# Latent attention: the products with the values in runs of six, behind the exponentials of three blocks of keys

## The chip, the cores and the metric

One Trainium2 chip, one of its cores. The metric is the time of one execution of the whole program on the device, in microseconds, as the median of several runs. The core has five engines that work side by side, each with its own queue of instructions in a fixed order: TensorE (PE in the rows; PEld is its loading of weights), VectorE (DVE), ScalarE (ACT), GpSimd (POOL) and SyncE (SP), whose queue issues the DMA transfers. An instruction starts when it stands first in its engine's queue and the semaphores that it waits for are there.

## The reference

Two transformer-like blocks over 512 latent and 256 context tokens of width 1024, in float32. The part that is changed is the attention of the first block's second layer: 16 heads, 512 queries, 768 keys, head width 96 for the scores and 64 for the values.

```python
def softmax_attention(q, k, v):
    s = jnp.einsum('bqhd,bkhd->bhqk', q, k).astype(jnp.float32) * ((QK_NOPE + QK_ROPE) ** -0.5)
    p = jax.nn.softmax(s, axis=-1)
    return jnp.einsum('bhqk,bkhd->bqhd', p.astype(v.dtype), v)
```

## The kernel before

The work is laid out with the keys on the partitions. The heads go in eight pairs (`p` = 0 to 7). `attend(p)` runs over six blocks of 128 keys; for each block and each head `i` of the pair it makes the transposed scores [128 keys, 512 queries] in one bank of PSUM by three products of split operands (high and low parts, lines 1607 to 1609), and ScalarE writes their exponentials (`act`, line 382) to one half of a buffer `pt` in SBUF. The two products with the values (line 1614) follow, one for each head. A product writes 64 partitions: the first head's the lower half of the bank `po`, the second head's the upper half. They sum over the blocks in `po`. The exponentials of the blocks are also added up (line 385): blocks 1, 4 and 5 into the buffer of block 0 on VectorE, block 3 into the buffer of block 2 on GpSimd. After the last block four products with a column of ones (line 1624, the "sum" below) give the row sums, VectorE takes the reciprocal (line 1627, 3.36 us) and multiplies `po` by it.

While a pair is attended to, `project(p + 1)` makes the next pair's operands from other banks: weights are split and multiplied (lines 430, 432, 435), queries and keys are split again, and a bound on each query's scores is found: 16 products (line 1583), each two of them followed by a reduction of 768 columns on VectorE (line 1584), then a small cast (line 1586) and eight transposing products (line 1590, 1x128 in the order) whose row enters the next pair's scores. Three of the eight banks belong to `attend` (one is `po`, two take scores by turns), five to the rest.

The lines are written in the order of the mathematics; a scheduler places the instructions on each engine by its own estimate of when operands are there, which is how the products of line 1583 and those of the projection come to stand between the score products. Once it has run, the order on each engine is fixed. A float32 product on 64 columns of the array is two MATMUL instructions in the trace, so the 96 products with the values are 192 instructions of 512 columns.

Of the kernel before, what the change touches and what calls it, by code (L numbers as in the profile page):

```python
# [11 lines left out]
AF = mybir.ActivationFunctionType  # L12
OP = mybir.AluOpType
# [3 lines left out]
TL, TC, TA = 512, 256, 768  # L17
# [343 lines left out]
class _K:  # L361
# [18 lines left out]

    def act(self, out, in_, func=AF.Copy, **kw):
        return self.nc.scalar.activation(out, in_, func, **kw)  # L382

    def tt(self, out, a, b, op, eng=None):
        return (eng or self.nc.vector).tensor_tensor(out, a, b, op=op)  # L385
# [1028 lines left out]
    def mla(self, a, vec):  # L1414
        nc, A, B, I = self.nc, self.A, self.B, self.I
        A.forget(9999)
        mm = nc.tensor.matmul
# [36 lines left out]
        acc = A.new([TA], top=True)  # L1454
# [18 lines left out]
        b = B.new()  # L1473
# [19 lines left out]
        sc = 96.0 ** -0.5  # L1493
# [102 lines left out]
        def attend(p, ops):  # L1596

            qh, ql, kh, kl = ops
            v = vs[p // 2]
            po = B.new()  # L1600
            acc = [None, None]
            for kb in range(6):
                ks = slice(128 * kb, 128 * kb + 128)
                pt = A.new([2, TL])
                for i in range(2):
                    b = B.new()
                    mm(b.a, kh.a[:97, i, ks], qh.a[:97, i, :], start=True, stop=False)  # L1607
                    mm(b.a, kl.a[:96, i, ks], qh.a[:96, i, :], start=False, stop=False)
                    mm(b.a, kh.a[:96, i, ks], ql.a[:96, i, :], start=False, stop=True)
                    self.act(pt.a[:, i, :], b.a, AF.Exp, scale=sc)  # L1610
                    b.free()
                for i in range(2):
                    h = 2 * (p % 2) + i
                    mm(po.a[64 * i:64 * i + 64, :], v.a[:, kb, 64 * h:64 * h + 64], pt.a[:, i, :], start=(kb == 0), stop=(kb == 5))  # L1614
                j = 1 if kb in (2, 3) else 0
                if acc[j] is None:
                    acc[j] = pt
                else:
                    self.tt(acc[j].a, acc[j].a, pt.a, OP.add, nc.gpsimd if j else None)
                    pt.free()  # L1620
            b = B.new()
            for j in range(2):
                for i in range(2):
                    mm(b.a[64 * i:64 * i + 64, :], self.ones.a[:, :64], acc[j].a[:, i, :], start=(j == 0), stop=(j == 1))
            self.free(acc)
            r = A.new([TL])
            nc.vector.reciprocal(r.a, b.a)
            b.free()
            self.tt(o.a[:, p, :], po.a, r.a, OP.mult)
            self.free([r, po, qh, ql])  # L1630
            if p % 2:
                v.free()
# [3 lines left out]
        for p in range(8):  # L1636
            nxt = project(p + 1) if p < 7 else None
            if p == 6:
                A.limit = 20480 // A.G
                self.wraw = [self.load(I["w1out"][n], "inner") for n in range(2, 2 + 6)]  # L1640
                A.limit = A.n
            B.cur = 3
            attend(p, ops)
            self.in_zone(0)
            ops = nxt
# [1093 lines left out]
```

## Time and profile before

| what | value |
|---|---|
| median of 3 runs | 3063.88 us (3060.31 to 3068.25) |
| the profiled execution, own time | 3062.72 us |
| its span, first to last instruction | 3061.0 us |
| TensorE busy in the span | 94% |
| VectorE, ScalarE, GpSimd busy | 56%, 32%, 10% |
| mean granted TensorE clock, share of full speed | 0.964 |

The attention over the eight pairs lies between 1246 and 1510 us of the span. Busy time counts an engine as busy while one of its instructions runs; for TensorE the ends of pipelined products are modelled, so that a product of 512 columns is shown with 0.39 to 0.40 us while the next starts some 0.23 us after it. Distances between starts say more than durations.

### The profile page before, as it was taken

To read this page: it belongs to the slowest core of one execution; us is meant where nothing else is said; L and a number is where in the kernel's file an instruction comes from. 1 tells how busy PE (TensorE), PEld (TensorE's weight loads), DVE (VectorE), ACT (ScalarE), POOL (GpSimd) and SP (SyncE) were. 2 spreads that over 40 slices of the span, in tenths; PEclk is the share of its full clock that TensorE was granted. 3 is DMA by queue.
4 is the path that set the end of the run, shared out by engine and by line. 5 is a ranking of instruction groups with operands and counts; after the bars stand their busy time and mean duration, and the time that the engine had idled before them with its cause. 6 is when DMAs were issued, how large, how long until landed. Compare 5 with 4: busy or idle time off the path is not lost.

```text
span 3061.0 us, 43732 instructions
## 1 busy us (share of the span) xinstructions
PE 2879.1 (94%) x17880; PEld 2056.7 (67%) x17880; DVE 1703.4 (56%) x2733; ACT 982.3 (32%) x1605; POOL 297.6 (10%) x271
## 2 busy tenths in 40 slices
PE   7989999999999989999999999979798898999997
PEld 4776557888888877555588787877585564344443
DVE  5856547686575354656664784368856943121113
ACT  5522334511211256333453522254322323010011
POOL 0134310000000010111100000010301311000000
PEclk9999999999999999999999999989898887999999
DMA  6334362366465131001222222213113135999998
GB/s 217 103 109 123 117 198 71 124 232 201 134 234 184 34 118 42 23 26 42 90 84 84 82 90 70 89 36 124 63 50 104 48 132 189 399 409 409 409 409 295
DMA packets 170585, 458.99 MB, mean 150 GB/s; under 512 B 20320, under 2 KB 52704, under 8 KB 170000
## 3 DMA queue, kind: packets, MB, share of 16 engines
q1 hardware_dynamic: 170384, 456.19, 42.6%
q8 instruction: 140, 2.29, 0.3%
q14 instruction: 61, 0.50, 0.1%
HBM read 441.35 MB, written 14.78 MB: 149 GB/s over the span
## 4 chain that ended last, share of the span: by engine, by line
PE 69%; DVE 10%; DMA 5%; issue 4%; ACT 3%; POOL 1%; SPq 0%; DVEq 0%; ACTq 0%; POOLq 0%
PE ps L430 13%; PE ps L432 13%; PE ps L435 13%; PE ps L2596 9%; DVE mem L385 5%; ACT mem L382 3%; PE ps L1614 3%; PE ps L2579 2%; DVE mem L388 1%; DMA mem<-in_wadt_dram 1%; PE ps L606 1%; PE ps L1607 1%; PE ps L1770 1%; PE ps L1583 1%; POOL mem L385 1%
## 5 line engine op out<-in xcount | busy, mean ns | idle before, releaser
L382 ACT ACTIVATE mem<-mem 128x1024 fp32r<-128x1024 f32 (+16 forms) x802 | 543.5, 707 | 876.0 <-PE ps L435 224.0
L385 DVE TENSOR_TENSOR mem<-mem,mem 128x1024 fp32r<-128x1024 f32 (+13 forms) x595 | 508.5, 871 | 380.6 <-ACT mem L382 188.0
L382 ACT ACTIVATE mem<-ps 128x512 f32<-128x512 f32 (+8 forms) x607 | 313.1, 529 | 1026.5 <-PE ps L435 327.1
L430 PE MATMUL ps<-mem,mem 128*128 128x512 f32 (+3 forms) x1991 | 598.2, 357 | 14.8 <-ACT mem L382 10.2
L432 PE MATMUL ps<-mem,mem 128*128 128x512 f32 (+2 forms) x1906 | 567.5, 353 | 1.0 <-DVE mem L385 0.9
L435 PE MATMUL ps<-mem,mem 128*128 128x512 f32 (+2 forms) x1977 | 416.3, 351 | 0.0
L430 PEld LDWEIGHTS ps<-mem,mem 128*128 128x128 f32 (+2 forms) x1991 | 338.7, 189 | 86.6 <-ACT mem L382 17.0
L432 PEld LDWEIGHTS ps<-mem,mem 128*128 128x128 f32 (+1 forms) x1906 | 325.2, 188 | 59.9 <-issue 5.9
L435 PEld LDWEIGHTS ps<-mem,mem 128*128 128x128 f32 (+1 forms) x1977 | 322.7, 189 | 56.2 <-issue 4.1
L2596 PE MATMUL ps<-mem,mem 128*64 128x512 f32 x1344 | 308.4, 599 | 1.1 <-ACT mem L382 0.5
L432 PE MATMUL ps<-mem 128*128 128x512 f32 (+1 forms) x814 | 272.2, 364 | 1.3 <-POOL mem L385 0.9
L430 PE MATMUL ps<-mem 128*128 128x512 f32 (+1 forms) x729 | 254.4, 373 | 11.8 <-ACT mem L382 7.9
L385 POOL TENSOR_TENSOR mem<-mem 128x256 f32<-128x256 f32 (+4 forms) x72 | 96.1, 1336 | 1706.5 <-ACT mem L382 1382.7
L385 DVE TENSOR_TENSOR mem<-mem,ps 128x512 f32<-128x512 f32 (+5 forms) x234 | 128.9, 582 | 202.6 <-PE ps L2596 103.4
L385 DVE TENSOR_TENSOR mem<-mem 128x256 f32<-128x256 f32 (+19 forms) x347 | 186.1, 543 | 76.9 <-ACT mem L382 39.0
L2596 PEld LDWEIGHTS ps<-mem,mem 128*64 128x64 f32 x1344 | 106.4, 137 | 177.5 <-issue 164.6
L385 POOL TENSOR_TENSOR mem<-mem,mem 128x512 f32<-128x512 f32 (+6 forms) x104 | 141.4, 1371 | 537.6 <-ACT mem L382 427.5
L385 DVE TENSOR_TENSOR mem<-ps,mem 128x512 f32<-128x512 f32 (+6 forms) x196 | 123.0, 643 | 99.4 <-PE ps L1107 35.4
L432 PEld LDWEIGHTS ps<-mem 128*128 128x128 f32 x814 | 152.5, 194 | 30.2 <-issue 4.4
L435 PE MATMUL ps<-mem 128*128 128x512 f32 (+3 forms) x743 | 171.1, 360 | 0.0
L430 PEld LDWEIGHTS ps<-mem 128*128 128x128 f32 x729 | 139.0, 195 | 44.2 <-ACT mem L382 13.0
L388 DVE SCALAR_TENSOR_TENSOR mem<-ps,mem 128x256 f32<-128x256 f32 (+1 forms) x232 | 114.5, 532 | 73.5 <-PE ps L435 73.2
(301 smaller groups left out, 2930.2 us busy)
## 6 DMA issues: line engine op xcount, KB each, us to landing
mem<-in_eg_dram SPq DMA_DIRECT2D x128, 512.0 KB, 10.2
mem<-in_eu_dram SPq DMA_DIRECT2D x128, 512.0 KB, 10.2
mem<-in_ed_dram SPq DMA_DIRECT2D x128, 512.0 KB, 10.2
mem<-in_wadt_dram SPq DMA_DIRECT2D x96, 512.0 KB, 4.4
mem<-in_wup_dram SPq DMA_DIRECT2D x44, 512.0 KB, 3.6
mem<-in_wgate_dram SPq DMA_DIRECT2D x44, 512.0 KB, 3.5
mem<-in_wdown_dram SPq DMA_DIRECT2D x40, 512.0 KB, 3.5
mem<-in_w2in_dram SPq DMA_DIRECT2D x35, 512.0 KB, 3.7
```

Of the source, the lines that this page charges most:

```text
L382: return self.nc.scalar.activation(out, in_, func, **kw)
L385: return (eng or self.nc.vector).tensor_tensor(out, a, b, op=op)
L388: return self.nc.vector.scalar_tensor_tensor(out, a, s, b, op0=op0, op1=op1)
L430: mm(o, w(0, k), acts[k][0][:, ts], start=(k == 0), stop=False)
L432: mm(o, w(0, k), acts[k][1][:, ts], start=False, stop=False)
L435: mm(o, w(1, k), acts[k][0][:, ts], start=False, stop=(k == nk - 1))
L606: nc.tensor.matmul(b.a[32 * q:32 * q + 32, :], cs.a[:, k, :], raw.a[:, j * 512:(j + 1) * 512], start=(k == 0), stop=(k == 7))
L1583: mm(b.a[:, t0:t1], qh.a[:96, i, 128 * c:128 * c + 128], kh.a[:96, i, t0:t1], start=True, stop=True)
L1607: mm(b.a, kh.a[:97, i, ks], qh.a[:97, i, :], start=True, stop=False)
L1614: mm(po.a[64 * i:64 * i + 64, :], v.a[:, kb, 64 * h:64 * h + 64], pt.a[:, i, :], start=(kb == 0), stop=(kb == 5))
L2579: mm(b.a[:, :256], ht.a[:, c, fs], o, start=(c == 0), stop=(c == 3))
L2596: mm(bk.a[64 * i:64 * i + 64, 512 * n:512 * n + 512], lhs(k, i), w[i][:, 512 * n:512 * n + 512], start=(k == 0), stop=(k == 7))
```

## The change

For each half of a pair's six blocks, all six score blocks (three blocks, two heads) and their exponentials now come first. Then the six products with the values are issued one behind the other, the two heads by turns, at high priority for the scheduler, and each of the six gets an explicit dependency on the last of the six exponentials (`behind`). The additions of the exponentials come after the six products. No instruction is added or taken away.

```diff
+    def behind(self, ins, other):
+
+        self.tc.add_manual_dep(ins.ins, other.ins.name, mybir.DependencyInfo(mybir.DependencyClass.Sync, mybir.DependencyReason.DATA),
+                               reason="in one run")
...
-            for kb in range(6):
-                ks = slice(128 * kb, 128 * kb + 128)
-                pt = A.new([2, TL])
-                for i in range(2):
...
-                    self.act(pt.a[:, i, :], b.a, AF.Exp, scale=sc)
-                    b.free()
-                for i in range(2):
-                    h = 2 * (p % 2) + i
-                    mm(po.a[64 * i:64 * i + 64, :], v.a[:, kb, 64 * h:64 * h + 64], pt.a[:, i, :], start=(kb == 0), stop=(kb == 5))
-                j = 1 if kb in (2, 3) else 0
...
+            for k0 in range(0, 6, 3):
+                pts = []
+                for kb in range(k0, k0 + 3):
...
+                        e = self.act(pt.a[:, i, :], b.a, AF.Exp, scale=sc)
+                        b.free()
+                    pts.append(pt)
+
+                with self.tc.high_priority():
+                    for kb, pt in zip(range(k0, k0 + 3), pts):
+                        for i in range(2):
+                            h = 2 * (p % 2) + i
+                            m = mm(po.a[64 * i:64 * i + 64, :], v.a[:, kb, 64 * h:64 * h + 64], pt.a[:, i, :], start=(kb == 0), stop=(kb == 5))
+                            self.behind(m, e)
+                for kb, pt in zip(range(k0, k0 + 3), pts):
+                    j = 1 if kb in (2, 3) else 0
...
```

Lines shift: the scores' products stand in lines 1614 to 1616 of the changed kernel, those with the values in 1625, the sum in 1637, the bound's products in 1588 (of before 1583) and its transposes in 1595, the projection's in 435, 437 and 440.

TensorE's queue in the first half of pair 4, before: two score products, products of line 1583 for the next pair's bound between them, and the two heads' products with the values apart from each other.

```order
L1607 MATMUL ps<-mem_80,mem_76 128x512
L1608 MATMUL ps<-mem_80,mem_76 128x512
L1583 MATMUL ps<-mem_76,mem_80 128x256
L1609 MATMUL ps<-mem_80,mem_76 128x512
L1614 MATMUL ps<-mem_7557,mem_68 64x512
L1583 MATMUL ps<-mem_76,mem_80 128x512
L1583 MATMUL ps<-mem_76,mem_80 128x256
L1614 MATMUL ps<-mem_7557,mem_68 64x512
L1607 MATMUL ps<-mem_80,mem_76 128x512
```

The same place in the changed kernel, from the last score product of the sixth head (the first row) on; the next two rows of scores belong to the seventh.

```order
L1616 MATMUL ps<-mem_80,mem_76 128x512
L1614 MATMUL ps<-mem_80,mem_76 128x512
L1588 MATMUL ps<-mem_76,mem_80 128x512
L1588 MATMUL ps<-mem_76,mem_80 128x256
L1615 MATMUL ps<-mem_80,mem_76 128x512
L1625 MATMUL ps<-mem_7557,mem_68 64x512 x4
L1625 MATMUL ps<-mem_68 64x512 x2
L1588 MATMUL ps<-mem_76,mem_80 128x512
L1588 MATMUL ps<-mem_76,mem_80 128x256
L1588 MATMUL ps<-mem_76,mem_80 128x512
L1588 MATMUL ps<-mem_76,mem_80 128x256
```

The six products with the values, one or two to a place before, stand in one piece, with two score products and two of the bound's between them and the last score product they need.

TensorE's queue at the end of the same pair, before, from the scores of the twelfth and last head to the sum (1624).

```order
L1607 MATMUL ps<-mem_80,mem_76 128x512
L1608 MATMUL ps<-mem_80,mem_76 128x512
L1609 MATMUL ps<-mem_80,mem_76 128x512
L430 MATMUL ps<-mem_76 128x512
L1614 MATMUL ps<-mem_7557,mem_68 64x512 x2
L432 MATMUL ps<-mem_76 128x512
L430 MATMUL ps<-mem_76 128x256
L430 MATMUL ps<-mem_76 128x512
L432 MATMUL ps<-mem_76 128x256
L432 MATMUL ps<-mem_76 128x512
L1624 MATMUL ps<-mem_7557,mem_64 64x512 x2
L1624 MATMUL ps<-mem_68,mem_64 64x512 x2
```

And in the changed kernel, from the last score product on.

```order
L1616 MATMUL ps<-mem_80,mem_76 128x512
L435 MATMUL ps<-mem_76 128x512
L437 MATMUL ps<-mem_76 128x512
L435 MATMUL ps<-mem_76 128x512
L437 MATMUL ps<-mem_76 128x256
L437 MATMUL ps<-mem_76 128x512
L440 MATMUL ps<-mem_76,mem_80 128x256
L440 MATMUL ps<-mem_76,mem_80 128x512
L1625 MATMUL ps<-mem_7557,mem_68 64x512 x6
L1637 MATMUL ps<-mem_7557,mem_64 64x512 x2
L1637 MATMUL ps<-mem_68,mem_64 64x512 x2
```

The second run stands right in front of the sum, behind seven products of the projection; before, a pair of products with the values stood there, and five of the projection between it and the sum.

The SP queue behind the last pair, before (`w1out` is the weight of the product that follows attention, `wgate` and `cx` belong to later work).

```order
L400 DMA mem_7557<-in_w1out_dram 128x1024 x2
L400 DMA mem_9545<-in_wgate_dram 128x1024
L2138 DMA mem_64<-in_cx_dram 128x256 x3
L400 DMA mem_7557<-in_w2in_dram 128x1024
```

And in the changed kernel.

```order
L405 DMA mem_7557<-in_w1out_dram 128x1024
L405 DMA mem_9545<-in_wgate_dram 128x1024
L2151 DMA mem_64<-in_cx_dram 128x256
L405 DMA mem_7557<-in_w1out_dram 128x1024
L2151 DMA mem_64<-in_cx_dram 128x256 x4
```

The second of the two `w1out` transfers has moved behind a `wgate` transfer and one of `cx`.

## Rows read from the trace of the kernel before

**Rows 1.** the page: the span, TensorE, and the chain that ended last by line.

```profile
span 3061.0 us, 43732 instructions
...
PE 2879.1 (94%) x17880; PEld 2056.7 (67%) x17880; DVE 1703.4 (56%) x2733; ACT 982.3 (32%) x1605; POOL 297.6 (10%) x271
...
PE ps L430 13%; PE ps L432 13%; PE ps L435 13%; PE ps L2596 9%; DVE mem L385 5%; ACT mem L382 3%; PE ps L1614 3%; PE ps L2579 2%; DVE mem L388 1%; DMA mem<-in_wadt_dram 1%; PE ps L606 1%; PE ps L1607 1%; PE ps L1770 1%; PE ps L1583 1%; POOL mem L385 1%
```

**Rows 2.** busy time by engine of two stretches: us (instructions); granted clock; DMA.

```profile
1317.00:1388.00 71.00, 70.73 (x265) 38.59 (x264) 43.09 (x49) 25.71 (x44) 12.30 (x11) 1.00 0.09 27
1388.00:1459.00 71.00, 70.37 (x266) 38.56 (x266) 43.19 (x48) 25.11 (x43) 12.81 (x11) 1.00 0.14 45
```

**Rows 3.** groups of instructions by line from 1240 to 1510 us.

```profile
L1614 PE MATMUL ps<-mem,mem 128*64 128x512 f32 x168 | 77.9, 629 | 1.0 <-ACT mem L382 0.8
...
L1624 PE MATMUL ps<-mem,mem 128*64 128x512 f32 x64 | 15.5, 605 | 0.5 <-DVE mem L385 0.5
...
L1614 PE MATMUL ps<-mem 128*64 128x512 f32 x24 | 11.2, 618 | 0.0
```

**Rows 4.** the timeline, TensorE and ScalarE, 1424.2 to 1429.3 us: start, duration in us.

```profile
1424.26 0.50 PE L1607 MATMUL ps<-mem,mem 97*128 97x512 f32 x1
...
1424.60 0.40 PE L1608 MATMUL ps<-mem,mem 96*128 96x512 f32 x1
...
1425.19 0.39 PE L1609 MATMUL ps<-mem,mem 96*128 96x512 f32 x1
...
1425.67 0.60 ACT L382 ACTIVATE mem<-ps 128x512 f32<-128x512 f32 x1 [1.85 <-PE ps L1609]
...
1425.77 0.40 PE L1608 MATMUL ps<-mem,mem 96*128 96x512 f32 x1
...
1426.01 0.40 PE L1609 MATMUL ps<-mem,mem 96*128 96x512 f32 x1
...
1426.34 1.07 PE L1614 MATMUL ps<-mem,mem 128*64 128x512 f32 x2
...
1427.34 0.97 PE L1583 MATMUL ps<-mem,mem 96*128 96x512 f32 x4
...
1428.24 1.07 PE L1614 MATMUL ps<-mem,mem 128*64 128x512 f32 x2
```

**Rows 5.** the timeline of TensorE around one sum, 1407 to 1410 us.

```profile
1407.72 1.94 PE L1624 MATMUL ps<-mem,mem 128*64 128x512 f32 x8
1409.59 0.97 PE L435 MATMUL ps<-mem,mem 128*128 128x256 f32 x4
```

**Rows 6.** the waits in 1246 to 1508 us: total us, times, longest.

```profile
PEld ps L1614 <- ACT mem L382: 27.2, 70, 0.9
```

**Rows 7.** the timeline of GpSimd, VectorE and TensorE, 1293 to 1297 us.

```profile
1293.67 2.35 POOL L385 TENSOR_TENSOR mem<-mem 128x1024 f32<-128x1024 f32 x1 [12.63 <-issue]
1293.70 2.35 DVE L1586 CAST mem<-mem 128x8 fp32r<-128x8 f32 x1
...
1296.10 0.64 PE L1590 MATMUL ps<-mem,mem 128*1 128x128 f32 x8 [1.01 <-DVE mem L1586]
```

**Rows 8.** the timeline of the SP queue at the end of attention.

```profile
1493.20 8.48 SPq L400 DMA_DIRECT2D mem<-in_w1out_dram  x2
1501.73 0.42 SPq L400 DMA_DIRECT2D mem<-in_wgate_dram  x1
1506.24 1.28 SPq L2138 DMA_DIRECT2D mem<-in_cx_dram  x3
```

**Rows 9.** the timeline of TensorE, 1472 to 1484 us, idle time in brackets.

```profile
1472.76 1.56 PE L1614 MATMUL ps<-mem,mem 128*64 128x512 f32 x4 [0.51 <-ACT mem L382]
...
1483.61 0.80 PE L1607 MATMUL ps<-mem,mem 97*128 97x512 f32 x1 [3.46 <-DVE mem L1627]
```

**Rows 10.** the stretches around and behind these two, columns as in 2.

```profile
1471.80:1478.20 6.40, 5.17 (x16) 1.84 (x15) 4.29 (x6) 3.50 (x7) 0.00 (x0) 1.00 0.02 2
...
1483.60:1489.20 5.60, 5.59 (x11) 2.49 (x11) 1.38 (x2) 1.82 (x3) 0.00 (x0) 0.50 0.26 94
```

More of the change, by code (lines that the diff above doesn't have):

```diff
@@ L1601, in attend @@
             acc = [None, None]
-            for kb in range(6):
-                ks = slice(128 * kb, 128 * kb + 128)
-                pt = A.new([2, TL])
-                for i in range(2):
[L1606 to L1609, printed above, removed]
-                    self.act(pt.a[:, i, :], b.a, AF.Exp, scale=sc)
-                    b.free()
-                for i in range(2):
-                    h = 2 * (p % 2) + i
-                    mm(po.a[64 * i:64 * i + 64, :], v.a[:, kb, 64 * h:64 * h + 64], pt.a[:, i, :], start=(kb == 0), stop=(kb == 5))
-                j = 1 if kb in (2, 3) else 0
[L1616 to L1620, printed above, removed]
+            for k0 in range(0, 6, 3):
+                pts = []
+                for kb in range(k0, k0 + 3):
+                    ks = slice(128 * kb, 128 * kb + 128)
+                    pt = A.new([2, TL])
+                    for i in range(2):
+                        b = B.new()
+                        mm(b.a, kh.a[:97, i, ks], qh.a[:97, i, :], start=True, stop=False)
+                        mm(b.a, kl.a[:96, i, ks], qh.a[:96, i, :], start=False, stop=False)
+                        mm(b.a, kh.a[:96, i, ks], ql.a[:96, i, :], start=False, stop=True)
+                        e = self.act(pt.a[:, i, :], b.a, AF.Exp, scale=sc)
[3 more added lines that the diff above has]
+                    for kb, pt in zip(range(k0, k0 + 3), pts):
+                        for i in range(2):
+                            h = 2 * (p % 2) + i
[3 more added lines that the diff above has]
+                    j = 1 if kb in (2, 3) else 0
+                    if acc[j] is None:
+                        acc[j] = pt
+                    else:
+                        self.tt(acc[j].a, acc[j].a, pt.a, OP.add, nc.gpsimd if j else None)
+                        pt.free()
```

## The prediction

> **What bounds the kernel now.** The page first: TensorE is busy 94% of the span, and the chain that ended last runs mostly over its products [rows 1]. The products with the values (line 1614) hold 3% of that chain, the scores' first product 1%; so the change touches a small part, but a part on the path. Next the busy time by stretch: in the two stretches of 71 us that each cover two pairs, TensorE is busy over 70 us at full clock, VectorE 43 us, ScalarE 25 to 26 us, GpSimd 12 to 13 us [rows 2]. Attention is bound by TensorE's queue, and time saved there is saved at the end as long as the other engines keep up.
>
> Then the groups by line: the products with the values are busy 77.9 + 11.2 = 89.1 us for 192 instructions, the eight sums 15.5 us for 64 [rows 3]. Per instruction that is 0.46 us against 0.24 us, for the same shape, 64 columns of the array and 512 moving columns. The timeline says why. In the sum, eight instructions of two heads by turns take from 1407.72 to 1409.59, 1.87 us [rows 5]. One product with the values that stands alone, two instructions, keeps TensorE from 1426.34 to 1427.34, 1.00 us, and the second head's, after four other products, again 1.00 us from 1428.24 [rows 4]. So instructions of the two heads run side by side, those of one head do not. In TensorE's order before, 34 of the 96 products stand alone and 31 times the two heads' stand together (34 + 62 = 96), where the second head's has to wait for an exponential of its own: TensorE's loading of weights waits for ScalarE 70 times, 27.2 us in all, in part behind products that still run [rows 6].
>
> **The change part by part.** *Side by side.* Busy time of a run grows from 1.07 us (two steps of one head) to 1.94 us (four steps of two heads) [rows 4, 5], so a further step costs (1.94 - 1.07)/2 = 0.435 us. A run of six products is twelve instructions, six steps: 1.07 + 4 x 0.435 = 2.81 us. Sixteen such runs are 45.0 us, against 89.1: 44.1 us less. Each run's busy time overhangs the next start by 0.07 us (1.07 shown, 1.00 to the next start [rows 4]); 65 runs become 16, so 49 x 0.07 = 3.4 us of this was never TensorE's time. 40.7 us remain.
>
> *Changing over.* From one score product to the next it is 0.24 us (1425.77 to 1426.01); from the last one into the run it is 0.33 us (1426.01 to 1426.34), and the first product after a run holds 0.34 us (1424.26 to 1424.60) [rows 4]. A run costs 0.09 + 0.10 = 0.19 us beside its own steps. 49 runs fewer: 9.3 us.
>
> *The sum joins the second run* (the order at the end of pair 4). It loses its own changing over, 0.19 us, and its slot goes from 1.87 us to four steps, 1.74 us: 0.32 us, eight times 2.6 us.
>
> That is 40.7 + 9.3 + 2.6 = 52.6 us gross. Against it stand four new waits.
>
> *The last exponential.* Behind the last score product of the sixth head it takes 0.39 us to its end, then 0.09, the exponential 0.60, and 0.07 to the product: 1425.19 to 1426.34, 1.15 us [rows 4]. 0.24 us are the product's own slot, so other products must fill 0.91 us. In the changed order two score products and two of the bound's (0.24 + 0.24 + 0.24 + 0.12) fill 0.84 in the first run of pairs 1 to 6, and four to seven products of the projection fill all of it in the second run of pairs 0 to 5. Uncovered: 0.4 us once in pair 0, 0.1 six times, 0.2 in pair 7, and 0.9 us in the second runs of pairs 6 and 7, where nothing stands between. Sum 3.0 us. What is queued behind the waiting product (the next head's third score product, the bound's products) waits with it, and VectorE's first addition waits for the run's first two products, since it writes into block 0's exponentials. Both have slack: the sums of exponentials are needed only at line 1624, two blocks' additions later.
>
> *Two banks for scores.* Before, products with the values stood between every two heads. Now six heads' scores come in a row, and the third head's needs the first one's bank, free 1.15 us after its last product's start. TensorE would be there after four slots, 4 x 0.23 = 0.92 us: 0.23 us short. One product between covers it. In the order some 17 of 96 heads have none, most in pair 7 (nine), where there is no next pair to project: 17 x 0.23 = 3.9 us. The other bound is 80 x 0.23 = 18.4 us (96 heads less the 16 behind a run), if fillers don't help.
>
> *The bound's chain on VectorE.* Reductions, additions and the cast come closer together. The nearest row for a bad case: the cast took 2.35 us, as long as a GpSimd addition that began with it, and the transposing products waited 1.01 us for it [rows 7]. GpSimd's addition of block 3 now begins later, near the cast in each pair. I take 0.8 us for six pairs (pair 0 has its wait already), 4.8 us, between 0 and 1.5 us each (9 us).
>
> *The transfers behind attention.* The `w1out` transfers were issued at 1493.2 and 1501.7 (8.48 us for the two issues), `cx` at 1506.2 [rows 8]. The second now stands behind a `wgate` and one `cx`; if those still wait, it comes 4.5 us later against work that comes earlier. I take 2 us, between 0 and 8. A late second block is covered by the products with the first, and by the last pair's reciprocal, on which TensorE waits anyway (3.46 us behind the pair before [rows 9]).
>
> Holding three blocks of exponentials needs more buffers; no row shows a product or exponential that waits for one, so nothing; without that cover, each run would wait for one addition.
>
> New waits: 3.0 + 3.9 + 4.8 + 2 = 13.7 us. Net 52.6 - 13.7 = 38.9 us. On the profiled execution's own 3062.72 us (span and 1.7 us around it) that gives 3023.8, so **3024 us**; the median shown, 3063.88, is 1.2 us above it, less than the spread of its runs. Whatever follows attention starts as much earlier: TensorE is nearly always busy there too.
>
> **The rivals.** *The exponentials set the pace.* The two banks, the chain and the transfers all cost their upper bounds: 3.0 + 18.4 + 9 + 8 = 38.4 us, net 14.2 us, 3048 us; with half of the excess over my values, 3036. For it: before, a product with the values stood behind every second head, so no row shows six heads in a row on two banks. Against: ScalarE is busy 25 of 71 us [rows 2], and would be at some 42% in a stretch shortened to 61. The Trainium skill says in "TensorEngine Tiling (Array Packing)", section Performance Considerations, PSUM Bottleneck, that packing the array speeds up TensorE but not the emptying of PSUM, which may then bound. By that page the time is this rival's 3048 us; ScalarE's share above speaks against it here, the two score banks for it.
>
> *The heads do not overlap in a run.* If the products with the values stayed serial, each run would be twelve single steps, 1.07 + 10 x 0.435 = 5.4 us, 16 of them 86.7 us against 89.1. Gross 2.4 - 3.4 + 9.3 + 2.6 = 10.9 us, less 13.7: 3065 us, no change. For it: only the sum shows eight in a row. Against: its operands have the same shape and place.
>
> *Slower: the clock.* Waiting for a whole group could leave TensorE idle long enough for its clock to fall. After 3.46 us idle it did: the next 5.6 us ran at a granted 0.50, the lower of the two levels, 1.2 GHz; a wait of 0.51 us left the full clock in the stretch around it [rows 9, 10]. Such a wait costs 3.5 us and half of the 5.6 us that follow, 6.3 us. It decides if it strikes at ten of the sixteen runs, 63 us; at all of them it is 101 us, 3062.7 - 52.6 + 101 = 3111 us. It needs exponentials 3 us late, and the longest wait of these products now is 0.9 us [rows 6].
>
> *The change gains more*: only the 3.0 us of the first wait are lost, 3013 us.
>
> **How the numbers follow.** My forecast, 3013 to 3033 us, 0.67; the pace of the exponentials, 3033 to 3048, 0.17; still less lost, below 3013, 0.06; no overlap 0.05; the clock 0.03; a mixture of small harms around no change 0.02. What a measurement here can tell from no change is 0.3%, 9 us. Faster by more: 0.67 + 0.17 + 0.06 = 0.90; same 0.06; slower 0.04. The range, 3011 to 3042 us, leaves out the end of the pace rival and the small cases.
>
> **What would show it.** Right: line 1625 busy near 45 us for 192 instructions, in runs of twelve with the sum behind every second; pairs 29 to 31 us long where they were 35.5. The waits of line 1625 for ScalarE few and under 1 us. Wrong: runs near 5 us (no overlap); scores' products more than 0.3 us apart (banks); waits of line 1595 for the cast over 1 us in most pairs (the chain); a granted clock under 0.9 in attention (clock); TensorE idle behind the last sum (transfers).

## The result and the profile after

The changed kernel takes 3028.44 us (median; 3024.39 to 3031.81), the one before 3062.85 us (3060.31 to 3068.25): a ratio of 0.9878, 95% interval 0.9861 to 0.9895. Forecast were 3024 us and 3011 to 3042. The two profiled executions differ by 33.8 us (3062.72 and 3028.96).

The page after answers to [rows 1]: TensorE's busy share is the same 94%, of a shorter span. The products with the values, now line 1625, hold 1% of the chain, where line 1614 held 3%.

```profile
span 3027.3 us, 43733 instructions
...
PE 2845.5 (94%) x17880; PEld 2061.2 (68%) x17880; DVE 1704.7 (56%) x2733; ACT 980.8 (32%) x1605; POOL 298.6 (10%) x271
...
PE ps L435 13%; PE ps L440 13%; PE ps L437 13%; PE ps L2609 9%; DVE mem L390 5%; ACT mem L382 2%; PE ps L2592 2%; PE ps L1625 1%; DVE mem L393 1%; DMA mem<-in_wadt_dram 1%; PE ps L611 1%; DMA mem<-in_ed_dram 1%; DMA mem<-in_eu_dram 1%; PE ps L1783 1%; POOL mem L390 1%
```

The groups of 1240 to 1480 us answer to [rows 3]: 41.5 + 6.2 = 47.7 us for the same 192 instructions, in place of 89.1. An instruction still lasts 0.6 us; two of them now lie over each other.

```profile
L1625 PE MATMUL ps<-mem,mem 128*64 128x512 f32 x168 | 41.5, 620 | 1.4 <-ACT mem L382 1.4
...
L1637 PE MATMUL ps<-mem,mem 128*64 128x512 f32 x64 | 15.1, 592 | 0.0
...
L1625 PE MATMUL ps<-mem 128*64 128x512 f32 x24 | 6.2, 597 | 0.0
```

One run in TensorE's timeline, to be held against [rows 4]: twelve instructions begin at 1309.58, and the next product begins at 1312.31. That is 2.73 us for six products of two heads, where one product alone took 1.00 us.

```profile
1309.26 0.40 PE L1615 MATMUL ps<-mem,mem 96*128 96x512 f32 x1
1309.58 1.08 PE L1625 MATMUL ps<-mem 128*64 128x512 f32 x4
1310.49 1.89 PE L1625 MATMUL ps<-mem,mem 128*64 128x512 f32 x8
1312.31 0.97 PE L1588 MATMUL ps<-mem,mem 96*128 96x512 f32 x4
```

From the first score product of pair 2 to that of pair 4 it is now 59.8 us, from there to pair 6 60.3, where it was 70.9 twice. In two stretches cut a little longer than that TensorE idles for some 2 us each, where in [rows 2] it idled for 0.3 to 0.6.

```profile
1292.90:1354.10 61.20, 59.33 (x273) 37.88 (x274) 45.65 (x49) 27.06 (x47) 13.08 (x13) 1.00 0.11 33
1354.10:1415.60 61.50, 59.26 (x274) 37.68 (x272) 44.98 (x47) 24.67 (x42) 13.02 (x12) 1.00 0.11 35
```

The waits of 1246 to 1480 us name that idle time (us in total, times, longest). PE is TensorE itself; PEld is its loading of weights, whose waits partly lie beside products that still run.

```profile
PEld ps L1614 <- ACT mem L382: 8.3, 28, 0.5
PEld ps L1595 <- DVE mem L1591: 6.8, 6, 1.6
PEld ps L1625 <- ACT mem L382: 6.3, 16, 1.4
PE ps L1595 <- DVE mem L1591: 4.7, 6, 1.2
...
PE ps L1614 <- DVE mem L1640: 3.5, 1, 3.5
...
PE ps L1625 <- ACT mem L382: 1.4, 2, 0.7
```

**Where the time went.** To keep attention apart from the rest I take one stretch in every kernel: from the end of TensorE's first 6,200 instructions (the next starts at 1195.94 us before, ahead of attention) to its 10,480th from the end (1520.23 us before, behind it). Before it takes 324.3 us, after 284.7: 39.6 us less. Outside the stretch the same program drifts from one execution to the next, as a run of the unchanged kernel shows below, so the experiments are read by this stretch beside their medians. It is good to about 2 us. Part of what differs in it is the clock: 10.3 us of it ran at a granted 0.50 before, 13.7 in the second profile of the unchanged kernel, 17.0 after.

### The profile page after: what moved, and what is told of

The parts are those of the page before. It is cut to its first block, busy times and chain, and to the rows that moved or that the text cites. A ratio compares the mean times of both kernels' runs of the same rounds, so it can differ in the third digit from the quotient of the medians.

```text
span 3027.3 us, 43733 instructions
## 1 busy us (share of the span) xinstructions
PE 2845.5 (94%) x17880; PEld 2061.2 (68%) x17880; DVE 1704.7 (56%) x2733; ACT 980.8 (32%) x1605; POOL 298.6 (10%) x271
## 4 chain that ended last, share of the span: by engine, by line
PE 68%; DVE 10%; DMA 5%; issue 4%; ACT 2%; POOL 1%; SPq 0%; DVEq 0%; ACTq 0%; POOLq 0%
PE ps L435 13%; PE ps L440 13%; PE ps L437 13%; PE ps L2609 9%; DVE mem L390 5%; ACT mem L382 2%; PE ps L2592 2%; PE ps L1625 1%; DVE mem L393 1%; DMA mem<-in_wadt_dram 1%; PE ps L611 1%; DMA mem<-in_ed_dram 1%; DMA mem<-in_eu_dram 1%; PE ps L1783 1%; POOL mem L390 1%
## 6 DMA issues: line engine op xcount, KB each, us to landing
mem<-in_eg_dram SPq DMA_DIRECT2D x128, 512.0 KB, 10.2
mem<-in_eu_dram SPq DMA_DIRECT2D x128, 512.0 KB, 10.2
mem<-in_ed_dram SPq DMA_DIRECT2D x128, 512.0 KB, 10.2
```

## The experiments

Median us of the whole kernel, ratio to before with its 95% interval, and the stretch:

| | median | ratio | stretch |
|---|---|---|---|
| before | 3062.85 | | 324.3 |
| after | 3028.44 | 0.9878 [0.9861, 0.9895] | 284.7 |
| before again | 3066.84 | 0.9999 [0.998, 1.0017] | 322.3 |
| no dependency | 3064.55 | 1.0002 [0.9988, 1.0015] | 323.5 |
| heads apart in a run | 3039.39 | 0.9917 [0.9894, 0.9941] | 294.9 |
| one head per run | 3068.02 | 1.0008 [0.9996, 1.0021] | 323.4 |
| runs of one block | 3040.25 | 0.9921 [0.9892, 0.995] | 294.9 |
| runs of six blocks | 3033.57 | 0.9906 [0.9874, 0.9938] | 293.8 |
| third block on VectorE | 3018.65 | 0.9849 [0.9822, 0.9875] | 276.7 |
| cast on ScalarE | 3017.82 | 0.9846 [0.9826, 0.9866] | 277.9 |
| cast on ScalarE, again | 3015.61 | 0.9846 [0.9821, 0.987] | 277.4 |
| four banks | 3030.1 | 0.9877 [0.9856, 0.9898] | 286.4 |
| cast on ScalarE, four banks | 3019.28 | 0.9849 [0.9826, 0.9871] | 280.2 |
| after again | 3028.51 | 0.988 [0.9859, 0.99] | 285.2 |

My theory was that of the prediction: the two heads lie side by side on TensorE's columns, and fewer runs mean fewer changings between kinds of product. The first rival was that the longer uninterrupted order gains and the overlap is little.

**The order alone, without the dependency.** The products are issued in the new order and with the same priority, but don't wait for the last exponential.

```diff
-                            self.behind(m, e)
```

> The code in runs of six and at high priority, but no product waits for the last exponential. The scheduler then places the products as they come: 30 alone, 33 in twos. By the theory this is the kernel before again: 63 runs, 30 x 1.0 + 33 x 1.0 to 1.65 + 63 x 0.19 us, so 3050 to 3063 us. Rival (the grouping of the scores and the later additions bring the gain): near 3030 us.

3064.55 us. There are 33 runs of two products and 30 of one, and the group by line of 1240 to 1515 us is back at the 77.9 + 10.7 us of before. So the wait makes the runs; without it the scheduler places each product where it takes its own exponential to be there.

```profile
L1625 PE MATMUL ps<-mem,mem 128*64 128x512 f32 x168 | 77.9, 629 | 1.4 <-ACT mem L382 1.2
...
L1625 PE MATMUL ps<-mem 128*64 128x512 f32 x24 | 10.7, 618 | 0.0
```

**The unchanged kernel once more.**

> The kernel before, unchanged, with a profile of its own: how far the same stretches of work shift from one profiled execution to the next. Theory: up to 2 to 3 us at single places, as the shift of 2 us ahead of attention in the changed kernel's profile already shows; so the 4 us that went between the end of attention and the end of the program there are such shifts. Rival (later stages lose time by the change): shifts under 1 us.

3066.84 us. Its profiled execution has a span 16.4 us longer than the first one's, and yet an attention stretch 2.0 us shorter: what differs lies outside. This is the size of the drift that single executions carry.

**The heads apart, within a run.**

```diff
-                    for kb, pt in zip(range(k0, k0 + 3), pts):
-                        for i in range(2):
+                    for i in range(2):
+                        for kb, pt in zip(range(k0, k0 + 3), pts):
```

> The six products of a run stand by head: three of the first, then three of the second. Runs, dependency and place are those of the changed kernel. Theory (the two heads' instructions run side by side only where they stand by turns): a run takes eleven steps in place of six, 1.07 + 9 x 0.435 = 4.99 us busy against 2.81, so 16 x 2.2 = 35 us more than the changed kernel, about 3063 us, no gain left. Rival (the gain comes from fewer changings over and fewer waits for exponentials): within 3 us of the changed kernel, about 3029 us, and the 192 instructions busy near 45 us.

3039.39 us, where I had expected no gain. The timeline shows why.

```profile
1314.61 1.07 PE L1625 MATMUL ps<-mem 128*64 128x512 f32 x2
1315.52 0.59 PE L1625 MATMUL ps<-mem,mem 128*64 128x512 f32 x1
1315.53 0.64 PE L1625 MATMUL ps<-mem 128*64 128x512 f32 x1
1315.95 0.59 PE L1625 MATMUL ps<-mem,mem 128*64 128x512 f32 x1
1316.01 0.59 PE L1625 MATMUL ps<-mem 128*64 128x512 f32 x1
1316.38 1.94 PE L1625 MATMUL ps<-mem,mem 128*64 128x512 f32 x6
1318.25 0.97 PE L1588 MATMUL ps<-mem,mem 96*128 96x512 f32 x4
```

In the program all six instructions of the first head stand ahead of the second's. In the trace they form two chains, each a step of about 0.43 us apart: one from 1314.61, the other from 1315.53 (in this run the form "mem" alone marks block 0 of either head, two instructions each). The second head began 0.92 us behind the first, when only three of the first's six had started. The run takes 3.64 us, between the 2.73 of side by side and the 5.4 that I had priced for single steps. So this edit did not take the overlap away, and could not test it.

**One head per run.** This one can: a run holds three products of one head, and scores stand between the runs.

```diff
-                for kb in range(k0, k0 + 3):
-                    pt = A.new([2, TL])
-                    for i in range(2):
+                pts = [A.new([2, TL]) for _ in range(3)]
+                for i in range(2):
+                    for kb, pt in zip(range(k0, k0 + 3), pts):
...
-                with self.tc.high_priority():
-                    for kb, pt in zip(range(k0, k0 + 3), pts):
-                        for i in range(2):
+                    with self.tc.high_priority():
+                        for kb, pt in zip(range(k0, k0 + 3), pts):
```

> Same number of changings between scores and values as one run of two heads by blocks, but a run holds three products of one head only, so nothing can lie side by side in it: 32 runs of three per pair count instead of 16 runs of twelve instructions. Theory (most of the gain, 40.7 of 52.6 us, is the two heads lying side by side on TensorE's columns): three products of one head take about 1.3 us, what the six of two heads take together is 2.7, so 32 runs take about the time of the products of before, the attention keeps only what fewer changings give (33 changings instead of 65), and the time is 3052 to 3066 us. Rival (the gain is the changings and the longer wait-free runs, and the side by side is little): 3028 to 3040 us.

3068.02 us, just above the range expected: no gain is left, and the rival falls. My own expectation priced a run wrongly. Three products of one head take not 1.3 us but 2.72, the time of six of two heads (1494.63 to 1497.35), so 32 runs take 86.9 us. At 0.19 us each the 33 changings that this version saves (39 runs in place of 72) should have left 6.3 us all the same, less the 1.8 us that the runs themselves grew; the stretch shows 0.9. The clock took some of it, 17.1 us at a granted 0.50 against 10.3 before; the rest lies within what the stretch is good for, and the gain by fewer changings is not shown by this run.

```profile
1494.63 2.79 PE L1621 MATMUL ps<-mem,mem 128*64 128x512 f32 x6
1497.35 0.50 PE L1613 MATMUL ps<-mem,mem 97*128 97x512 f32 x1
```

**The length of a run.** One block per run (48 runs of two products), and all six (8 runs of twelve).

```diff
-            for k0 in range(0, 6, 3):
+            for k0 in range(0, 6, 1):
...
-                for kb in range(k0, k0 + 3):
+                for kb in range(k0, k0 + 1):
```

> One block of keys to a run: 48 runs of two products, each behind the second head's exponential. Side by side, but with 48 changings over. Theory (both terms as sized): 48 runs of 1.00 us and 0.19 us for the change, seven sums apart, 73 us in place of the changed kernel's 61 us, so some 12 us slower than it, 3040 us, if the waits cost the same 14 us. Rival A (longer runs are what counts, since each wait for an exponential is paid once per run): 48 waits in place of 16, above 3050 us. Rival B (only side by side counts): 3030 us.

3040.25 us. All 48 runs are side by side, most in 1.01 us, and the group's busy time is 46.2 + 6.5 us. Against before this is the overlap nearly alone, with 17 runs fewer: 29.4 us of the stretch. About half of that is not won from products that stood alone. The 30 runs of two products without a sum took 49.1 us before, 1.0 to 2.7 each, since the second head's product waited for an exponential of its own; at 1.01 us they would be 30.3. From the first start of each run, the sums included, to the next other product, TensorE spends 72.4 us in 55 runs, where the change spends 62.3 in 16. These 10.2 us and 39 changings at 0.19 us are what longer runs save, 17.6 us; the stretch shows 10.2 of them. Long runs also bring the waits for banks that are measured below (2.7 us); the rest of the difference I have not traced. The wait for the cast is here too (5.7 us in five pairs), so it does not come from long runs.

> One run of twelve products per pair once all six blocks' exponentials are there: 8 runs instead of 16. Theory by slots (a run of two takes 1.12 us, of six products of each 2.73 us, so about 0.26 to 0.3 us per run saved and one overhang less): products 1.3 to 2.5 us shorter, but the run ends with the last exponential and the sums and the reciprocal stand right behind it; 3026 to 3031 us. Rival (twelve tiles of exponentials held at once and the bank of the values held longer delay the next pair's bounds): 3031 to 3045 us.

3033.57 us. The runs themselves do what the slots promised: 5.30 us where nothing joins them, twice 2.65. The time lies in the rival's range, but what is lost is a wait that neither theory priced. All additions of exponentials now begin with the one run, and the sum stands right behind it, so TensorE waits for VectorE in each of the eight pairs:

```profile
PE ps L1637 <- DVE mem L390: 14.3, 8, 3.6
...
PE ps L1595 <- DVE mem L1591: 0.7, 1, 0.7
```

**The cast.** In the changed kernel the transposing products (line 1595) wait in six pairs for a cast of 8 numbers per partition. In pair 6 it shows as follows (start, duration, and idle time in brackets):

```profile
1435.33 2.36 POOL L390 TENSOR_TENSOR mem<-mem 128x1024 f32<-128x1024 f32 x1 [20.85 <-ACT mem L382]
...
1435.73 1.98 DVE L1591 CAST mem<-mem 128x8 fp32r<-128x8 f32 x1
...
1437.77 1.01 PE L1595 MATMUL ps<-mem,mem 128*1 128x128 f32 x8 [1.25 <-DVE mem L1591]
...
1441.70 4.21 PE L1625 MATMUL ps<-mem,mem 128*64 128x512 f32 x12 [0.69 <-ACT mem L382]
```

The cast ends at 1437.71, GpSimd's addition at 1437.69. Two edits test that, each from one side: the addition of the fourth block goes to VectorE, or the cast goes to ScalarE.

```diff
-                        self.tt(acc[j].a, acc[j].a, pt.a, OP.add, nc.gpsimd if j else None)
+                        self.tt(acc[j].a, acc[j].a, pt.a, OP.add)
```

> The one addition per pair that ran on GpSimd goes to VectorE, so the short cast of the bounds meets no GpSimd addition. Theory (the cast takes about 2 us instead of 0.1 because the addition on GpSimd runs at the same time, and TensorE waits for it 4.7 us in six pairs, and loses half-rate clock behind it in pair 6, some 2.5 us): 3021 to 3026 us, no PE wait of more than 0.5 us on L1591's cast. Rival (the wait only moves: VectorE's own addition of 1024 elements stands ahead of the cast, reduces come later and the bounds with them): 3026 to 3032 us.

```diff
-            nc.vector.tensor_copy(mr.a, m.a)
+            self.act(mr.a, m.a)
```

> The cast of the bounds goes from VectorE to ScalarE, the addition stays on GpSimd. Theory (the cast is stretched by GpSimd's addition through what VectorE and GpSimd share): the cast on ScalarE lasts under 0.4 us and the wait of 4.7 us in six pairs shrinks to under 2, time 3022 to 3027 us. Rival (ScalarE has exponentials queued ahead of the cast, so the wait stays as long with another name): 3027 to 3031 us.

3018.65 and 3017.82 us, both faster than I had expected. With the addition on VectorE the view of line 1591 gives its casts 0.157 us at least, 0.167 in the median, 0.590 at most; in the changed kernel the median was 1.319:

```profile
L1591 DVE CAST mem<-mem x7: 157/167/590, 1254.7 to 1435.1; 128x8 fp32r<-128x8 f32 x7
```

With the cast on ScalarE the addition on GpSimd still lasts 2.39 us, but the cast takes 0.20 and the transposing products come without idle time. It is now an addition on VectorE that is stretched, to 1.85 us from 1.23, and no product waits for it there:

```profile
1429.62 2.39 POOL L390 TENSOR_TENSOR mem<-mem 128x1024 f32<-128x1024 f32 x1 [20.11 <-DVE mem L1589]
...
1430.15 0.20 ACT L382 ACTIVATE mem<-mem 128x8 fp32r<-128x8 f32 x1
...
1430.87 0.65 PE L1595 MATMUL ps<-mem,mem 128*1 128x128 f32 x8
...
1431.23 1.85 DVE L390 TENSOR_TENSOR mem<-mem 128x1024 f32<-128x1024 f32 x1 [1.25 <-issue]
```

Both edits take the wait away and shorten the stretch alike, so the cause is the two instructions together, not either engine's load. The Trainium skill gives the mechanism in "SBUF — State Buffer", section Who interferes with whom: VectorE and GpSimd share a pair of ports to the buffer, a cast can claim both of VectorE's pairs, and the later of the two blocks fully until the other ends. The ends 0.02 us apart agree with it.

**The banks.** Four of the eight banks for attention instead of three.

```diff
-        B.zone = [0] * 5 + [3] * 3
+        B.zone = [0] * 4 + [3] * 4
```

> The changed kernel with four of the eight PSUM banks for attention (three for scores beside the one of the values, or two beside values and sum) and four for the projection, in place of three and five. Theory (the score products wait for one of two banks, priced at 3.9 us in the prediction, and the first scores of the last pair wait 3.5 us for the reciprocal that holds a bank): waits of L1614 for ScalarE fall from 8.3 us to under 3 and the 3.5 us wait goes, 3020 to 3026 us. Rival (TensorE is fed by other work there, and the projection with four banks waits instead): 3026 to 3034 us.

> The cast of the bounds on ScalarE (3017.8 us by itself) and four banks for attention together. Theory (two separate waits, so the gains add): 3009 to 3015 us, faster than both kernels. Rival (the projection with four banks waits for its own copies out of PSUM, which also run on ScalarE, in front of the cast): 3016 to 3025 us.

3030.1 us, no gain, and 3019.28 together with the cast on ScalarE, no better than the cast by itself: in the time of the program the two gains do not add. In the first of them line 1614's waits for ScalarE did fall, from 8.3 us and 28 times to 4.1 and 6, and the 3.5 us behind the reciprocal went. At that place two waits came instead, since with values and sum of pair 6 and the values of pair 7 in three of the four banks, only one is left for scores:

```profile
1453.02 0.50 PE L1614 MATMUL ps<-mem,mem 97*128 97x512 f32 x1 [0.69 <-ACT mem L382]
...
1454.73 0.50 PE L1614 MATMUL ps<-mem,mem 97*128 97x512 f32 x1 [0.75 <-ACT mem L382]
```

That still leaves 2 us of gain there, while the stretch is 1 to 2 us longer. Cut at the first score product, the stretch shows where the gain went (us; two numbers are two profiles; with four banks up to nine products more come behind the cut, which makes both differences look smaller):

| | ahead of the first score product | from it on |
|---|---|---|
| after | 45.4, 46.0 | 239.3, 239.2 |
| four banks | 53.2 | 233.1 |
| cast on ScalarE | 45.1, 45.1 | 232.7, 232.3 |
| cast on ScalarE, four banks | 52.9 | 227.3 |

From the first scores on four banks gain 5 to 6 us, with and without the cast on ScalarE, so inside attention the two gains do add. About 3 us of it are the clock's: 6.8 us of that part run at a granted 0.50 in place of 13.0 and 14.0, and with the cast on ScalarE 3.4 in place of 10.0 and 9.9. The projection of the first pair, alone with its four banks, takes them back: its bound's products wait longer for VectorE's reductions (from 1200 to 1252 us, four banks first, then the changed kernel), and in both versions 20.5 us ahead of the first scores run at a granted 0.50, where in the changed kernel it is 4.0 and 6.4.

```profile
PE ps L1588 <- DVE mem L1589: 4.9, 5, 1.2
...
PE ps L1588 <- DVE mem L1589: 1.4, 2, 1.0
```

The fourth bank given over only behind that first projection was not tried.

**The change and the better version side by side.** These two ran together with the two of the banks.

> The changed kernel itself, beside the others on the same chip. Expected: 3025 to 3032 us, slower than the version with four banks and the cast on ScalarE by 10 us or more if both waits are real, and ratio to before 0.986 to 0.990.

> The cast on ScalarE again, on the same chip as the changed kernel. Theory (GpSimd's addition stretches the cast on VectorE, and TensorE's waits and the half-rate stretch behind the sixth of them cost together 6 to 8 us): faster than the changed kernel by 6 to 10 us. Rival (the two executions drifted apart elsewhere, and only the 4.7 us of waits count): faster by 2 to 5 us.

3028.51 us (3027.34 to 3032.14) and 3015.61 us (3012.76 to 3026.99): no run of the one is as fast as any of the other. The cast on ScalarE beats both kernels, the changed one by 12.9 us here in the median, more than the 6 to 10 expected. The stretch accounts for 7.8 of them; what gives the rest, behind attention or in drift, stays open. With four banks besides it is 9.2 us, just short of the 10 expected.

## Why the prediction held, point by point

**Side by side and changing over** (40.7 + 9.3 + 2.6 = 52.6 us gross): right, in size too, though the changings are priced and not measured by themselves. From the first start of each run, the sums included, to the next other product, TensorE spent 103.65 us in 72 runs before and 62.29 in 16 after: 41.4 us. Another 56 changings at my 0.19 us are 10.6, together 52.0; and 1.4 us more were there, since one run of the 16 fell into a stretch of half clock (4.05 us in place of 2.63). The experiments with one head and with one block per run agree with the overlap as the larger part: without it 0.9 us are left, with it and short runs 29.4. What the changings give by themselves no run shows.

**The last exponential** (3.0): too much by 1.2. Measured as the excess of the slot ahead of a run over 0.33 us (a slot is the time from one product's start to the next one's), 1.0 and 0.8 us were lost in the second runs of pairs 6 and 7, for which I had taken 0.9 each; the other fourteen runs lost nothing, for which I had taken 1.2 in all.

**Two banks** (3.9): somewhat less. Ahead of 28 heads the slot is over 0.03 us longer than the usual 0.24 us, or 0.12 behind a short product, 3.8 us in all; six of them, 1.0 us, are only slots at half clock. 22 heads and 2.7 us remain, spread over all pairs but pair 1 and not mostly in pair 7. Four banks won it back inside attention and lost it again ahead of it.

**The cast** (4.8, between 0 and 9): the right mechanism, too small. The slots ahead of line 1595 are longer by 1.0, 0.7, 1.0, 0.7, 1.2 and 1.5 us, 6.0 us in six pairs, where I had 0.8 for each. With the two removals the stretch falls to 276.7, 277.9 and 277.4 us, on average 7.6 us under the mean of the two profiles of the changed kernel. The difference of 1.6 us is about what the clock cost, below. TensorE's own wait for the cast was over 1 us in one pair, not "over 1 us in most pairs", the sign of being wrong that I had named.

**The transfers behind attention** (2): nothing. Issued at 1460.89 and 1467.31, `w1out` came 32 and 34 us earlier than in [rows 8], the work at the end of the stretch 37. In the 82 us behind attention TensorE waits 1.7 us after and 0.9 before. The SP queue held them no longer than before, and the step that "if those still wait, it comes 4.5 us later" did not occur.

Together the new waits inside attention cost 1.8 + 2.7 + 7.6 = 12.1 us, where the sum had 11.7; 53.4 - 12.1 = 41.3 against 39.6 and, in the second profile, 39.1 measured, as close as the stretch is good for. That the sum of the waits came out so near is in part luck: the cast was 2.8 us too small, the other three together 4.4 us too large. The median lies 4.4 us above the forecast although attention gained what it should: the profiled execution gave 5.8 us back outside the stretch, and the unchanged kernel run again shows that such amounts come and go. When the two ran again beside the last four kernels, the medians were 3066.76 and 3028.51, 38.3 us apart.

**The rivals.** The pace of the exponentials: waits for ScalarE exist (8.3 and 6.3 us at the loading of weights), but TensorE itself idles only 1.8 us for them, and ScalarE is busy 27.06 of 61.20 us. So what the Trainium skill says in "TensorEngine Tiling (Array Packing)", section Performance Considerations, PSUM Bottleneck, which the prediction weighed, did not decide here; 22 heads of 96 run into it, and briefly. That the heads don't overlap is refuted. The clock struck once in attention beyond what it did before, not at ten runs: in the two windows 1437.8 to 1444.6 and 1451.4 to 1454.8 (busy time by engine, then granted clock) it is 0.50, together 10.2 us. Before, the records have 6.8 us of it at this end of attention, around the stretch of [rows 10]. 3.4 us more at half rate cost about 1.7 us. In the second profile of the unchanged kernel it is 3.4 us there, so the difference carries drift of its own.

```profile
1437.80:1444.60 6.80, 6.11 (x21) 3.21 (x23) 4.65 (x10) 3.24 (x5) 0.00 (x0) 0.50 0.08 21
...
1451.40:1454.80 3.40, 3.40 (x9) 2.58 (x8) 1.06 (x2) 1.82 (x3) 0.00 (x0) 0.50 0.46 151
```

## What to carry to other kernels

Products that fill half of TensorE's columns are worth issuing by turns between the halves, and a dependency on the last operand of a group is a cheap way to bring them together: it costs only what no other product fills, here 1.8 us of 16 waits. Make the group long enough to save changings and short enough that what hangs on its results (here the additions ahead of the sum) can still be spread. After such an edit look for short instructions on VectorE that have moved beside a long one on GpSimd: moving one of them to another engine gave a further fifth of what the change itself gave in attention (7.6 of 39.6 us).

## What the runs showed of the hardware

**TensorE starts products of the other column half ahead of their turn.** With six instructions for the lower half ahead of six for the upper, the seventh started at 1315.53, before the fourth at 1315.95. The Trainium skill says in "TensorE: Matmul & The Clock Gate", section The mechanism, that products start and end in the order of the program; this trace shows otherwise for starts across column halves, and the measurement decides. Nor does it hold for them that an instruction starts only when it stands first in its engine's queue, as the first section has it. How far ahead it reaches beyond these three I have not measured.

**The length of an idle stretch alone does not tell whether the clock falls.** After 1.25 us idle at 1437.77 the granted clock was 0.50, and after 1.26 us again in the second execution of the changed kernel. With the cast on ScalarE TensorE idled 1.40 us ahead of 1433.90, and the next 4.5 us ran at 1.00; it fell only behind the 3.46 us for the reciprocal:

```profile
1433.90 2.79 PE L1625 MATMUL ps<-mem,mem 128*64 128x512 f32 x12 [1.40 <-ACT mem L382]
...
1433.90:1438.40 4.50, 4.50 (x20) 1.34 (x20) 2.98 (x9) 1.30 (x3) 0.00 (x0) 1.00 0.31 88
1443.30:1450.10 6.80, 6.70 (x17) 4.73 (x15) 0.63 (x1) 3.37 (x6) 0.00 (x0) 0.50 0.24 77
```

My prediction's two points (0.51 us without a fall, 3.46 with one) suggested a boundary between them; these do not give one.
